# Trunk of two hybrid decoder layers: rows of `ar` copied on chip, loads kept back by a second planning run, another matmul order in the outer quarters

## The chip, the core and the metric

The kernel runs on one NeuronCore of a Trainium2 chip, as a single launch. The metric is the time of one execution on the device in microseconds. The core's engines are TensorE (PE; its weight loads are PEld), VectorE (DVE), ScalarE (ACT), GpSimd (POOL) and SyncE (SP). SyncE computes nothing here: it issues most of the DMAs, GpSimd issues the others.

## What is computed

One inference step of a trunk of two layers, for a prompt of 256 tokens and 8 sampled tokens (264 columns), model width 2048:

```python
h = rms_norm(x, norm_w)
z = jnp.einsum('btd,dc->btc', h, w_in)          # 2048 -> 7296 columns, all branches
y_a, ... = rwkv_time_mix(z_a, ...)              # A: 12 heads x 64, delta-rule state
y_b, ... = attention_branch(z_b, ...)           # B: dilated sliding windows, 12 heads x 64
y_c, ... = pool_branch(z_c, ...)                # C: causal mean pooling, 4 x 128 channels
y = x + jnp.einsum('btc,cd->btd', concat(y_a, y_b, y_c), w_out)
```

Branch A is a recurrence over tokens, `S = S * w + sa (kk * a)^T + v k^T`, read by `r`. The kernel computes it for the prompt in four chunks of 64 tokens. Outputs are the two activations, the recurrent states and the new key and value rows.

## The kernel before

**The stream.** All weights pass once through the core in float32. `stream` (L301) computes two output tiles of 128 columns at a time, a *pair*, for all 264 tokens. A pair has four *quarters* of the depth; for each quarter `load` (L294) brings 512 KB into `raw` (three buffers), ScalarE casts it to `hi` (two buffers, float32r) and VectorE forms the remainder `lo` (three buffers). A tile is then the sum of hi x xh, hi x xl (8 matmuls a quarter) and lo x xh (4 matmuls a quarter) in one PSUM bank `acc`. There are three such banks, so the second tile of a pair reuses the bank of the first tile of the pair before. In each quarter the order is: hi of tile 0, hi of tile 1, lo of tile 0, lo of tile 1. `scaled` (L327) evicts a finished bank on VectorE by a product with `rstd` into `z` (and `compb`), which releases it. There are 29 pairs or single tiles a layer for w_in, then 8 pairs for w_out in quarter order (2, 1, 3, 0).

**Branch A beside the stream.** `a_kdone` and `a_r` build the operands `bk` and `ar`: `ar` holds for each pair of heads, chunk and token 64 columns of r and 64 of minus kk, scaled by the decays. `a_solve` (L469) multiplies them into the masked blocks `gs`, stores these to the DRAM tensor `g_dram`, gathers the diagonal blocks (`xm`), and inverts 16x16 triangles on VectorE in 15 steps (`tm`, `rm`), with many small stores in between (`x_dram`, `ra_dram`, `rat_dram`, `rb_dram`, `rbt_dram`). L500 to L504 also store the second half of `ar` over those rows of `g_dram` where a head's block has no use for its own masked values. `invert` (L523) loads the pieces again and completes the inverse. `a_chain` then runs over the four chunks: `fetch` (L636) loads one chunk's `gs` (768 KB, two buffers) from `g_dram`, and `chunk` (L680) uses it as the weights of a product with `uv`; since the `ar` rows stand in `gs`, the state's part and the chunk's part are one matmul. Chunk 0 has no state and reads only the other rows of `gs`. Meanwhile the sampled tokens (`a_sample`) store and load rows through `sk_dram` and `sv_dram` (loads `svec`, `sval`).

**The order.** All instructions are first written down in program order; `Plan` then sets the order of each engine's queue. `Plan.run` (L1532) simulates a list schedule: for each engine the ready instruction with the longest remaining tail goes next, with estimated durations (`cost`), crossing times, buffers (`rings`: the tiles of one tag take their buffers in order) and a model of the DMA engines (`bus`, L1501). Each engine then executes its list in that order, and waits only for what it depends on. All SyncE DMAs, the weights of the stream among them, form one such list.

Of the kernel before, what the change touches and what calls it, by code (L numbers as in the profile page):

```python
# [19 lines left out]
P = 128  # L20
# [3 lines left out]
T = NP + NB  # L24
# [18 lines left out]
UROWS = (slice(0, 64), slice(64, 128))  # L43
# [60 lines left out]
class Trunk:  # L104
# [196 lines left out]
    def stream(self, w, c0, nt, xh, xl, order=(0, 1, 2, 3), begin=False):  # L301
        n = nt * P
        accs = [self.ps("acc") for _ in range(nt)]
        for q in order:
            if begin:
                self.first_x(q)
                xh, xl = self.xh, self.xl
            raw = self.early.pop(0) if self.early else self.load(w, c0, n, q)
            hi = self.wpool.tile([P, 4, 256], F32R, tag="hi", name=self.nm("hi"), bufs=2)
            lo = self.wpool.tile([P, 4, 256], F32R, tag="lo", name=self.nm("lo"), bufs=3)  # L310
            self.act(hi[:, :, :n], raw[:, :, :n])
            self.tt(lo[:, :, :n], raw[:, :, :n], hi[:, :, :n].bitcast(F32), ALU.subtract)
            parts = ((hi, xh), (hi, xl)), ((lo, xh),)
            for late, products in zip((False, True), parts):
                for t in range(nt):
                    cs = slice(t * P, (t + 1) * P)
                    for k4 in range(4):
                        k = 4 * q + k4
                        for i, (a, b) in enumerate(products):
                            first = q == order[0] and k4 == 0 and not late and i == 0  # L320
                            self.nc.tensor.matmul(accs[t][:, :T], a[:, k4, cs], b[k], start=first, stop=q == order[3] and k4 == 3 and late)  # L321
        return accs

    def project(self, tiles):
# [144 lines left out]
    def a_solve(self):  # L469
# [7 lines left out]
        for t0 in (0, 3):  # L477
            gs = [ap.tile([P, NH, P], F32, tag="gs", name=self.nm("gs"), bufs=2) for _ in UROWS]
# [8 lines left out]
            for par, g in enumerate(gs):  # L487
                g0 = par * 6 + t0
# [3 lines left out]
        n = 96  # L492
# [4 lines left out]
                         self.g_dram[r0:r0 + 32, 6 * par:6 * par + 6, :, c0:c0 + 32].rearrange("s t c x -> (t c) s x"))  # L497
        self.dma(self.x_dram, xm[:n, :1024])
        self.load_x()
        for par, hr in enumerate(UROWS):  # L500
            for t0 in (0, 3):
                g0 = par * 6 + t0
                self.dma(self.g_dram[hr, g0:g0 + 3].rearrange("p t c n -> p (t c) n")[:, :, 64:128],
                         self.ar[hr, t0:t0 + 3].rearrange("p t c n -> p (t c) n")[:, :, 64:128])  # L504
        view = lambda a: a[:n].rearrange("p (u x) -> p u x", u=2)[:, :, :512].rearrange("p u (s t) -> p u s t", t=32)[:, :, :, :16]
        X, R = view(xm), view(rm)
        self.nc.vector.memset(rm, 0.0)
# [128 lines left out]
    def fetch(self, cidx):  # L636

        gs = self.apool.tile([P, NH, P], F32, tag="gs", name=self.nm("gs"), bufs=2)
        self.dma(gs, self.g_dram[:, :, cidx, :])
        return gs  # L640

    def inverses(self):
# [684 lines left out]
def width(a, first=1):  # L1327
    n = 1
    for _, c in list(a.ap)[first:]:
        n *= c  # L1330
    return n


class Plan:


    def __init__(self, tc, bundles):
        self.tc = tc
        self.tiles = {t.name: t for t in tc.tiles}
        self.block = tc.nc.cur_bb.bb  # L1340
        self.masks = {}
        engine = lambda i: ENGINES.get(str(i.engine).split(".")[-1])
        self.ins = [i for i in self.block.instructions if engine(i) and not type(i).__name__.startswith("BassTilePool")]
        self.eng = [engine(i) for i in self.ins]
        self.n = len(self.ins)
        self.dma = [type(i).__name__ == "InstDMACopy" for i in self.ins]
        self.stream = [type(i).__name__ == "InstMatmult" and self.tiles[list(i.outs)[0].bass_ap.tensor.name].tag.startswith("acc") for i in self.ins]
        self.first = self.stream.index(True)
        self.dur = [self.cost(i, e) for i, e in zip(self.ins, self.eng)]
        self.port = [self.shares(i, e) for i, e in zip(self.ins, self.eng)]  # L1350
        self.dependences()
        self.bundle(bundles)
        self.rings()
        gone, self.phases = [], []
        for i in self.block.instructions:
            if type(i).__name__.startswith("BassTilePool"):
                op, pool = self.boundary(i)
                if op == "alloc":
                    self.phases += [(pool, g) for g in gone]
                else:  # L1360
                    gone.append(pool)
# [139 lines left out]
    def bus(self, i):  # L1501
        o = list(i.outs)[0]
        run = min(a.ap[-1][1] * 4 if a.ap[-1][0] == 1 else 4 for a in list(i.ins) + list(i.outs))
        return width(o, 0) * 4 * (1.0 if run >= 512 else 2.0 if run >= 128 else 2.46 if run >= 64 else 8) / 360.0


    def tails(self, factor, hop, loose=()):
# [21 lines left out]
                tail[q] = max(tail[q], t)  # L1529
        return tail  # L1530

    def run(self, factor=1, hop=300, margin=200, batch=0, wait=0, switch=0, quiet=0, lead=1, dyn=()):  # L1532
        n, eng, preds, dma, dur, stream = self.n, self.eng, self.preds, self.dma, self.dur, self.stream
        spare = {t: d for t, r in self.ring.items() for m, d in dyn if t.split("_" + self.pool[r[0]])[0] == m}
        tail = self.tails(factor, hop, spare)
# [2 lines left out]
        feeds = {q for k in range(n) if stream[k] for q in preds[k]}  # L1538
# [3 lines left out]
        count = [0] * n  # L1542
# [19 lines left out]
        open_tiles = Counter(self.pool[t] for t in left)  # L1562
        live = set()
        parked = defaultdict(list)
        est = [0.0] * n
        names = ("PE", "SIDE", "DVE", "ACT", "POOL", "SP")
        ready = {e: [] for e in names}
        queue = lambda k: "SIDE" if eng[k] == "PE" and not stream[k] else eng[k]
        pending = [(0.0, k) for k in range(n) if count[k] == 0]
        heapq.heapify(pending)  # L1570
        free = {e: 0.0 for e in names if e != "SIDE"}
        hw = bus_free = now = 0.0
        start, fin, order = [0.0] * n, [0.0] * n, {e: [] for e in free}
# [33 lines left out]
        while done < n:  # L1607
            while pending and pending[0][0] <= now + 1e-9:
                _, k = heapq.heappop(pending)
                heapq.heappush(ready[queue(k)], (prio[k], k))  # L1610
            while release and release[0][0] <= now + 1e-9:
                _, t = heapq.heappop(release)
# [5 lines left out]
            for e in free:  # L1618
                if free[e] > now + 1e-9 or (e == "SP" and hw > now + 700):
                    continue  # L1620
                if e == "PE" and forced is not None:
                    k = forced
                elif e == "PE":
# [3 lines left out]
                    k = None  # L1627
                    if h:
                        go = side_on or h[0][0] < -2e9 or now - since >= wait or sum(dur[x[1]] for x in h) >= batch
                        if go:  # L1630
                            k = take(h)
# [3 lines left out]
                    if k is None:  # L1635
                        k = take(ready["PE"])
                        if k is None and h:
                            k = take(h)
# [3 lines left out]
                else:  # L1642
                    k = take(ready[e])
# [55 lines left out]
            c = [x for x in free.values() if x > now + 1e-9]  # L1699
# [6 lines left out]
            c = [x for x in c if x > now + 1e-9]  # L1706
# [71 lines left out]
def build(nc, shapes, depth=DEPTH):  # L1778
    ins = {n: nc.dram_tensor(f"in_{n}", s, F32, kind="ExternalInput").ap() for n, s in shapes.items()}
    outs = {n: nc.dram_tensor(f"out_{n}", s, F32, kind="ExternalOutput").ap() for n, s in _OUTS}  # L1780
    with tile.TileContext(nc, schedule_with_timeline_sim=True) as tc, ExitStack() as ctx:
        trunk = Trunk(ctx, tc, ins, outs, depth)
        trunk.run()
        plan = Plan(tc, trunk.bundles)
        plan.run(switch=105, margin=350, hop=180, factor=0.9, lead=25, quiet=60, dyn=[("a", 2)])
        plan.apply()


# [10 lines left out]
```

## Time and profile before

| | us |
|---|---|
| median of 3 runs | 1103.1 (1100.97 to 1105.57) |
| the profiled execution | 1103.96 |
| its span, first to last instruction | 1102.2 |
| TensorE busy | 1052.2 (95%) |
| VectorE busy | 854.1 (77%) |
| ScalarE busy | 545.0 (49%) |
| mean granted TensorE clock | 0.986 of full |
| moved by DMA | 223.64 MB, 203 GB/s over the span |

Matmuls are pipelined, so a busy time close to the span says that TensorE is seldom without work, not that each matmul is at its shortest. "L137 ACT hi<-raw" is an instruction of ScalarE from line 137 (a helper that many steps share) that writes tile `hi` and reads tile `raw`. A gap on an engine is shown as the idle time before an instruction with the instruction that ended it. A DMA on SyncE's queue has the time that its issue held the queue, not that of its transfer.

### The profile page before, as it was taken

How to read it: one execution, taken by the hardware profiler on the slowest of the kernel's cores; microseconds unless marked ns; L12 is line 12 of the kernel's file. 1: busy time of each engine (PE TensorE's matmuls, PEld its weight loads, DVE VectorE, ACT ScalarE, POOL GpSimd, SP SyncE). 2: the span in 40 equal slices, each digit the busy share in tenths (PEclk: the TensorE clock that was granted, in tenths of full speed). 3: DMA queues.
4: the chain of work that ended last, by engine and by line, in shares of the span. 5: the costliest groups of instructions: out<-in, count | busy, mean ns of one | idle time of the engine just before them, and what ended most of it. 6: DMA issues, size and time to landing. Idle time of an engine off the chain costs nothing. (4 is left out here: it accounts for less than half of the span.)

```text
span 1102.2 us, 24582 instructions
## 1 busy us (share of the span) xinstructions
PE 1052.2 (95%) x9802; PEld 1001.2 (91%) x9802; DVE 854.1 (77%) x1684; ACT 545.0 (49%) x934; POOL 128.3 (12%) x262
## 2 busy tenths in 40 slices
PE   9999998889999999999999999979999989999998
PEld 8899898789998888999999998978899988799998
DVE  7769977689997987765665799668999889776443
ACT  7646533354745563444455464324565555544332
POOL 0002300101122100000100032001021211100000
PEclk9999999899999999999999999998999999999999
DMA  8654478977568845677765545898865687456774
GB/s 278 201 170 149 135 248 224 240 191 226 149 204 243 278 127 192 190 221 219 236 215 182 169 144 171 229 240 238 225 202 166 194 266 230 160 169 190 232 225 146
DMA packets 154683, 223.64 MB, mean 203 GB/s; under 512 B 75984, under 2 KB 109152, under 8 KB 154552
## 3 DMA queue, kind: packets, MB, share of 16 engines
q1 hardware_dynamic: 146456, 195.94, 59.2%
q0 software_dynamic: 8112, 26.12, 7.2%
q8 instruction: 77, 1.26, 0.5%
q14 instruction: 38, 0.31, 0.1%
HBM read 198.55 MB, written 24.03 MB: 202 GB/s over the span
## 5 line engine op out<-in xcount | busy, mean ns | idle before, releaser
L137 ACT ACTIVATE hi<-raw 128x1024 fp32r<-128x1024 f32 (+1 forms) x296 | 309.8, 1047 | 400.9 <-PE acc L321 259.2
L321 PE MATMUL acc<-xh,hi 128*128 128x264 f32 x1824 | 473.3, 291 | 27.3 <-ACT hi L137 12.6
L140 DVE TENSOR_TENSOR lo<-raw,hi 128x1024 fp32r<-128x1024 f32 (+1 forms) x296 | 357.4, 1208 | 158.9 <-ACT hi L137 156.9
L321 PE MATMUL acc<-xl,hi 128*128 128x264 f32 x1824 | 472.0, 291 | 0.0
L321 PEld LDWEIGHTS acc<-xh,hi 128*128 128x128 f32 x1824 | 347.7, 191 | 36.6 <-ACT hi L137 14.3
L321 PEld LDWEIGHTS acc<-xl,hi 128*128 128x128 f32 x1824 | 348.4, 191 | 6.3 <-issue 4.2
L321 PE MATMUL acc<-xh,lo 128*128 128x264 f32 x1824 | 278.8, 290 | 0.4 <-DVE lo L140 0.4
L321 PEld LDWEIGHTS acc<-xh,lo 128*128 128x128 f32 x1824 | 243.8, 191 | 4.4 <-issue 1.2
L140 DVE TENSOR_TENSOR z<-acc,rstd 128x264 f32<-128x264 f32 (+1 forms) x112 | 50.8, 463 | 17.2 <-PE acc L321 15.3
L321 PE MATMUL acc<-mb,hi 128*128 128x264 f32 x384 | 54.4, 284 | 0.0
L321 PEld LDWEIGHTS acc<-mb,hi 128*128 128x128 f32 x384 | 49.9, 188 | 0.0
L321 PE MATMUL acc<-ml,hi 128*128 128x264 f32 x192 | 48.5, 284 | 0.0
L321 PE MATMUL acc<-mh,hi 128*128 128x264 f32 x192 | 48.4, 283 | 0.0
L351 POOL COPY zcol<-z 128x9 f32<-128x9 f32 x50 | 17.9, 360 | 189.1 <-DVE z L140 187.4
L321 PEld LDWEIGHTS acc<-mh,hi 128*128 128x128 f32 x192 | 36.1, 188 | 0.0
L321 PEld LDWEIGHTS acc<-ml,hi 128*128 128x128 f32 x192 | 36.1, 188 | 0.0
L321 PE MATMUL acc<-mc,hi 128*128 128x264 f32 x256 | 34.4, 285 | 0.1
L321 PEld LDWEIGHTS acc<-mc,hi 128*128 128x128 f32 x256 | 32.3, 188 | 0.6 <-DVE mc L140 0.5
L321 PE MATMUL acc<-mb,lo 128*128 128x264 f32 x192 | 31.1, 284 | 0.0
L321 PE MATMUL acc<-mh,lo 128*128 128x264 f32 x192 | 31.1, 284 | 0.0
L140 DVE TENSOR_TENSOR xs<-acc,res 128x264 f32<-128x264 f32 x32 | 13.7, 429 | 20.2 <-PE acc L321 20.1
L321 PEld LDWEIGHTS acc<-mh,lo 128*128 128x128 f32 x192 | 26.5, 188 | 0.0
(357 smaller groups left out, 1302.7 us busy)
## 6 DMA issues: line engine op xcount, KB each, us to landing
raw<-in_w_in SPq DMA_DIRECT2D x224, 512.0 KB
raw<-in_w_out SPq DMA_DIRECT2D x64, 512.0 KB
g_dram<-gs SPq DMA_DIRECT2D x8, 768.0 KB
gs<-g_dram SPq DMA_DIRECT2D x8, 768.0 KB
kc<-in_cache_k_w POOLq DMA_DIRECT2D x12, 512.0 KB, 7.3
qb<-q_dram SPq DMA_DIRECT2D x12, 512.0 KB
vc<-in_cache_v_w POOLq DMA_DIRECT2D x12, 512.0 KB, 4.6
s<-in_state_wkv POOLq DMA_DIRECT2D x12, 256.0 KB, 4.4
```

Of the source, the lines that this page charges most:

```text
L137: self.nc.scalar.activation(out, in_, func, **kw)
L140: self.nc.vector.tensor_tensor(out, a, b, op=op)
L321: self.nc.tensor.matmul(accs[t][:, :T], a[:, k4, cs], b[k], start=first, stop=q == order[3] and k4 == 3 and late)
L351: self.nc.gpsimd.tensor_copy(self.zcol[:, :, a], z[:, NP - 1:T])
```

## The change

There are three edits.

1. The four DMAs a layer that store `ar` into `g_dram` are gone. Instead, `fetch` copies the 64 columns from `ar` into the loaded `gs` on ScalarE, two copies a chunk, for chunks 1 to 3.
2. `Plan.run` can plan twice. With `ahead` the first run gives, for each DMA into SBUF that isn't a `raw` load, the earliest start among the instructions that read it; in the second run the DMA isn't ready until 12,000 ns before that. The estimate for transfers in runs of 512 to 1023 bytes rises from 1.0 to 1.25.
3. In `stream`, in the first and the last quarter of a pair, the matmuls are sorted by tile: hi and lo of tile 0, then hi and lo of tile 1. The two middle quarters stay as they were.

```diff
             parts = ((hi, xh), (hi, xl)), ((lo, xh),)
-            for late, products in zip((False, True), parts):
-                for t in range(nt):
-                    cs = slice(t * P, (t + 1) * P)
...
+            turns = [(late, t) for late in (0, 1) for t in range(nt)]
+            if q in (order[0], order[3]):
+                turns.sort(key=lambda x: x[1])
+            for late, t in turns:
+                cs = slice(t * P, (t + 1) * P)
...
         self.dma(self.x_dram, xm[:n, :1024])
         self.load_x()
-        for par, hr in enumerate(UROWS):
-            for t0 in (0, 3):
-                g0 = par * 6 + t0
-                self.dma(self.g_dram[hr, g0:g0 + 3].rearrange("p t c n -> p (t c) n")[:, :, 64:128],
-                         self.ar[hr, t0:t0 + 3].rearrange("p t c n -> p (t c) n")[:, :, 64:128])
...
         self.dma(gs, self.g_dram[:, :, cidx, :])
+        for par, hr in enumerate(UROWS):
+            if cidx:
+                self.act(gs[hr, 6 * par:6 * par + 6, 64:128], self.ar[hr, :, cidx, 64:128])
         return gs
...
+        self.first_out = [list(i.outs)[0].bass_ap.tensor.name if d else None for i, d in zip(self.ins, self.dma)]
+        self.after_load = defaultdict(list)
+        for k in range(self.n):
+            for q in self.preds[k]:
+                if self.dma[q] and self.first_out[q] in self.tag and not self.dma[k]:
+                    self.after_load[q].append(k)
...
-        return width(o, 0) * 4 * (1.0 if run >= 512 else 2.0 if run >= 128 else 2.46 if run >= 64 else 8) / 360.0
+        return width(o, 0) * 4 * (1.0 if run >= 1024 else 1.25 if run >= 512 else 2.0 if run >= 128 else 2.46 if run >= 64 else 8) / 360.0
...
+        self.hold = [0.0] * self.n
+        args = factor, hop, margin, batch, wait, switch, quiet, lead, dyn
+        if ahead:
+            self.once(*args)
+            for k, i in enumerate(self.ins):
+                if self.dma[k] and not self.feeds(k):
+                    self.hold[k] = max(0.0, min([self.start[q] for q in self.after_load[k]], default=0.0) - ahead)
+        return self.once(*args)
+
+    def feeds(self, k):
+        return self.tag[self.first_out[k]].startswith("raw") if self.first_out[k] in self.tag else False
...
-        est = [0.0] * n
+        est = list(self.hold)
...
-        pending = [(0.0, k) for k in range(n) if count[k] == 0]
+        pending = [(est[k], k) for k in range(n) if count[k] == 0]
...
-        plan.run(switch=105, margin=350, hop=180, factor=0.9, lead=25, quiet=60, dyn=[("a", 2)])
+        plan.run(ahead=12000, switch=105, margin=350, hop=180, factor=0.9, lead=25, quiet=60, dyn=[("a", 2)])
```

`once` is the former `run`. The transfers that part 1 removes have runs of 64 elements (256 bytes).

## Rows read from the trace of the kernel before

**Rows 1.** The page, busy time, share of the span and instructions of each engine
```profile
PE 1052.2 (95%) x9802; PEld 1001.2 (91%) x9802; DVE 854.1 (77%) x1684; ACT 545.0 (49%) x934; POOL 128.3 (12%) x262
```

**Rows 2.** Waits of TensorE: for whom, us in total, times, longest
```profile
PE acc L321 <- ACT hi L137: 12.6, 8, 4.3
PE acc L321 <- DVE z L140: 8.8, 13, 2.1
PE acc L321 <- DVE compb L140: 6.0, 5, 2.5
...
PE acc L321 <- DVE lo L140: 0.4, 1, 0.4
```

**Rows 3.** Windows: length, busy us of PE, PEld, DVE, ACT, POOL (x), clock, DMA share, GB/s
```profile
184.00:187.00 3.00, 2.98 (x14) 3.00 (x15) 2.93 (x6) 1.69 (x3) 0.00 (x0) 0.50 0.69 194
...
194.00:204.00 10.00, 5.35 (x34) 4.66 (x34) 2.43 (x6) 2.75 (x4) 0.86 (x2) 0.83 1.00 239
...
500.00:525.00 25.00, 25.00 (x209) 25.00 (x208) 15.91 (x23) 12.26 (x19) 2.70 (x5) 1.00 0.76 233
...
740.00:752.00 12.00, 7.96 (x43) 7.43 (x43) 6.89 (x11) 5.09 (x6) 1.08 (x2) 0.72 1.07 250
...
744.00:750.00 6.00, 5.03 (x23) 5.03 (x24) 4.12 (x4) 4.95 (x6) 0.54 (x1) 0.50 1.13 296
```

**Rows 4.** Timeline of TensorE: start, us, instruction, [idle before, who ended it]
```profile
180.34 0.39 PE L321 MATMUL acc<-xh,hi 128*128 128x264 f32 x1 [1.46 <-ACT hi L137]
...
184.03 0.56 PE L321 MATMUL acc<-xh,hi 128*128 128x264 f32 x1 [2.45 <-DVE compb L140]
...
202.33 0.59 PE L321 MATMUL acc<-xh,hi 128*128 128x264 f32 x1 [4.32 <-ACT hi L137]
...
727.17 0.36 PE L321 MATMUL acc<-xh,hi 128*128 128x264 f32 x1 [2.45 <-DVE compb L140]
...
744.97 0.59 PE L321 MATMUL acc<-xh,hi 128*128 128x264 f32 x1 [3.72 <-ACT hi L137]
```

**Rows 5.** Timeline of SyncE's queue, 174 to 198 us
```profile
174.40 1.46 SPq L155 DMA_DIRECT2D raw<-in_w_in  x1
...
176.38 3.50 SPq L155 DMA_DIRECT2D g_dram<-ar  x4
179.97 0.63 SPq L155 DMA_DIRECT2D raw<-in_w_in  x1
...
187.18 0.38 SPq L155 DMA_DIRECT2D raw<-in_w_in  x1
187.65 1.51 SPq L155 DMA_DIRECT2D gs<-g_dram  x2
189.25 5.42 SPq L155 DMA_DIRECT2D ra_dram<-rm  x2
...
196.13 1.50 SPq L155 DMA_DIRECT2D raw<-in_w_in  x1
```

**Rows 6.** Timeline of ScalarE in the same stretch, casts that waited for weights
```profile
179.23 1.06 ACT L137 ACTIVATE hi<-raw 128x1024 fp32r<-128x1024 f32 x1 [4.45 <-DMA raw<-in_w_in]
...
201.22 1.06 ACT L137 ACTIVATE hi<-raw 128x1024 fp32r<-128x1024 f32 x1 [8.38 <-DMA raw<-in_w_in]
```

**Rows 7.** Groups by line: shapes, count, busy us, mean ns, idle before
```profile
L137 ACT ACTIVATE uv<-st 64x384 f32<-64x384 f32 x12 | 6.3, 521 | 2.3 <-DVE st L140 2.0
...
L140 DVE TENSOR_TENSOR lo<-raw,hi 128x1024 fp32r<-128x1024 f32 (+1 forms) x296 | 357.4, 1208 | 158.9 <-ACT hi L137 156.9
```

**Rows 8.** Timeline of TensorE, first matmuls that read a fetched gs
```profile
238.19 0.92 PE L115 MATMUL a<-uv,gs 64*64 64x64 f32 x24
```

**Rows 9.** Waits of ScalarE's casts for TensorE
```profile
ACT hi L137 <- PE acc L321: 259.2, 153, 4.8
```

**Rows 10.** Timeline of TensorE, 908 to 920 us
```profile
912.77 0.39 PE L321 MATMUL acc<-xh,hi 128*128 128x264 f32 x1 [2.06 <-DVE z L140]
```

More of the change, by code (lines that the diff above doesn't have):

```diff
@@ L313, in stream @@
             parts = ((hi, xh), (hi, xl)), ((lo, xh),)
-            for late, products in zip((False, True), parts):
-                for t in range(nt):
-                    cs = slice(t * P, (t + 1) * P)
[L317 to L321, printed above, removed]
+            turns = [(late, t) for late in (0, 1) for t in range(nt)]
[3 more added lines that the diff above has]
+                cs = slice(t * P, (t + 1) * P)
+                for k4 in range(4):
+                    k = 4 * q + k4
+                    for i, (a, b) in enumerate(parts[late]):
+                        first = q == order[0] and k4 == 0 and not late and i == 0
+                        self.nc.tensor.matmul(accs[t][:, :T], a[:, k4, cs], b[k], start=first, stop=q == order[3] and k4 == 3 and late == 1)
         return accs
@@ L1530, in tails, with run, once @@
         return tail
-    def run(self, factor=1, hop=300, margin=200, batch=0, wait=0, switch=0, quiet=0, lead=1, dyn=()):
+    def run(self, factor=1, hop=300, margin=200, batch=0, wait=0, switch=0, quiet=0, lead=1, dyn=(), ahead=0):
+        self.hold = [0.0] * self.n
[8 more added lines that the diff above has]
+        return self.tag[self.first_out[k]].startswith("raw") if self.first_out[k] in self.tag else False
+    def once(self, factor, hop, margin, batch, wait, switch, quiet, lead, dyn):
         n, eng, preds, dma, dur, stream = self.n, self.eng, self.preds, self.dma, self.dur, self.stream
```

## Prediction

> **What bounds the kernel now.** I read the busy times first: TensorE is busy for 1052.2 of 1102.2 us, VectorE for 854.1, ScalarE for 545.0 [rows 1]. The kernel is therefore a TensorE kernel, and a change can only win time in the 50 us in which TensorE stands still and in stretches where its clock is low. Next I read TensorE's own waits [rows 2]: 12.6 us for the ScalarE cast `hi`, 8.8 and 6.0 us for the VectorE evictions `z` and `compb` that free an accumulator, and next to nothing (0.4 us) for `lo`. Third come the windows [rows 3], which tell where. In an undisturbed stretch TensorE runs 209 matmuls in 25 us, so one every 0.120 us, with the 16 DMA engines 0.76 busy. From 194 to 204 us it runs 34 in 10 us with the DMA share at 1.00, and from 740 to 752 us 43 in 12 us at 1.07: this is the same place in both layers, the triangular solve of branch A (pairs 29-30 and 31-32). I call it the crunch. Fourth, TensorE's timeline there [rows 4]: stalls of 1.46, 2.45 and 4.32 us in layer 0, of 2.45 and 3.72 us in layer 1, 14.4 us in all, mostly for `hi`.
>
> Why `hi` is late is read from ScalarE's timeline [rows 6]: it waited 4.45 and 8.38 us for weights (`raw`). Why the weights are late is read from SyncE's queue [rows 5], which issues every `raw` load in one line with all else. Its slices stand back to back: four `ar` stores take 3.50 us just ahead of the `raw` at 179.97; two `gs` loads (1.51 us) are followed by two small `ra` stores that hold the queue for 5.42 us, and the next `raw` goes out only at 196.13. The cast that needs it starts at 201.22 and TensorE at 202.33. The `gs` loads that stand in the way at 187.65 are first read by a matmul at 238.19 [rows 8], 50 us later.
>
> After the stalls the granted clock is 0.50, the 1.2 GHz level [rows 3]: 14 matmuls from 184 to 187 us, where 25 fit at the full rate (1.3 us lost), and 23 from 744.97 to 750, 5.03 us for what takes 2.75 (2.3 us lost). Layer 0 has a second dip like the latter behind the 4.32 us stall; I put it at 2.3 too. The crunch thus costs 14.4 + 5.9 = 20.3 us.
>
> **Part 1, `ar` by a copy.** Removed: eight stores of 192 KB, four a layer, 3.50 us of SyncE's queue each time [rows 5], and their DMA time. Added: for chunks 1 to 3, two ScalarE copies of 64x384 each, 12 in all. The same form exists (`uv<-st`, 521 ns [rows 7]): 12 x 0.521 = 6.3 us of an engine that is idle half the time. Bounds 0 (beside idle time) and 6.3 (all in front of a needed cast); nearer to 0, since ScalarE waited 259.2 us in 153 waits for TensorE to release a `hi` buffer [rows 9], 1.7 us each, so a copy of half a microsecond usually stands in such a wait. I take **+1**. It adds a wait: the copy waits for the landing of `gs`, and behind it on ScalarE stand the casts, for which TensorE waits. That is the slower rival below.
>
> **Part 2, loads kept back.** The planner runs once, and then no SBUF load but `raw` may go earlier than 12 us before its first reader started in that run. Stores have no hold. In the crunch this moves the eight `x` loads, `svec`, `sval` and the `gs` loads behind several `raw` loads. For `gs` one step more is needed: the first reader of chunk 0's is the matmul at 238, so it is held to about 226. Those of chunks 1 to 3 are first read by the new copy, which follows the landing at once, so their own hold is idle; but the two `gs` buffers are taken in order, so chunk 1's can't pass chunk 0's. Loads issued by GpSimd are held as well; its queue was no bottleneck at 128.3 us busy [rows 1]. The changed bus price (1.25 for runs of 512 to 1023 bytes) only shifts the order.
>
> What goes: with `ar`, `gs` and the small loads out of the way, the `raw` of 179.97 can go some 3.5 us and that of 196.13 some 10 us sooner, more than the stalls of 4.32 and 3.72 us. I count both and their two dips: 8.0 + 4.6 = **-12.6**. What stays: the stall of 1.46 us, whose `raw` was issued at 174.40, ahead of all that is removed, and the dip of 1.3 us. What is late next are the small stores, which keep their place.
>
> What comes: two `gs` loads of 768 KB near 226 us. At the 239 GB/s of the crowded window [rows 3] they are 6.4 us of all DMA engines a layer. The bounds are 0 (three `raw` buffers hide it) and 12.8 for both layers; SyncE's queue is emptier there, so I stay near the lower end: **+3**.
>
> The Trainium skill speaks against this part: "DMA: Bandwidth & Descriptors", Rules for kernel authors, says to issue a DMA early and wait for its semaphore late, so that its fixed cost overlaps with work. By that rule the two `gs` loads at 187.65 were placed well and part 2 would win nothing. The trace differs so far: the 5.42 us of queue behind them is the price of the early issue.
>
> **Part 3, tiles completed early.** In the first and last quarter of a pair the order hi t0, hi t1, lo t0, lo t1 becomes hi t0, lo t0, hi t1, lo t1. Tile 0's sum ends 8 matmuls sooner (12 before the end, not 4), and the next pair's second tile, which needs that buffer of three, starts after 12 matmuls and not 8. The eviction gets 12 x 0.120 = 1.44 us more. Behind one `lo` (1.21 us on VectorE [rows 7]) it now just gets through. The waits for `z` and `compb` are 14.8 us in 18 [rows 2]. Two of them are the 2.45 us in the crunch: 1.44 off each, **-2.9**. The other 16 sum to 9.9, 0.6 each, less than the slack but for the one of 2.06 us [rows 10], where 0.6 is left. At most 9.3 are to be had, at least 0, if the planner spends the slack on other work; I take **-5**, the middle, as some stand at a pair's start, where the order gives nothing.
>
> Its price: `lo` is wanted 0.96 us sooner in outer quarters. The cast runs ahead [rows 9], and TensorE waited for `lo` once, 0.4 us, in the crunch [rows 2]. Bounds 0 and 3.8 (two quarters in each crunch); **+0.4**. A `hi` buffer is released 4 matmuls (0.5 us) later in those quarters, inside the 1.7 us wait: 0.
>
> **Sum.** -12.6 - 2.9 - 5 + 1 + 3 + 0.4 = -16.1 us. The profiled execution took 1104.0 us (span 1102.2 and 1.8 around it), so 1087.9; from the median, 1103.1, it is **1087**. The profiled execution lies within the runs shown, 0.9 above their median.
>
> **Rivals.** (a) *The crunch stays.* Small stores (`sk`, `x_dram`, `ra`, `rb`, `rat`) keep SyncE's queue as full, and the weights are late as before. For it: the `raw` of 174.40 itself took 1.46 us to issue before any `ar` or `gs`. Against: the 5.42 us come right behind `gs`. This is also where the rule of the Trainium skill above would lead. Then only part 3 pays: 1103.1 - 7.9 + 4.4 = 1100.
> (b) *ScalarE is held by a late `gs`.* Six copies wait for a load that the planner believes landed; in order behind them stand the casts. Cover 1.7 us [rows 9]. If the loads come late as `raw` did in the crunch, by 8.38 us [rows 6], each costs 6.7, six 40, and against the gain 1127; at 6.6 us late it is 4.9 each, 29 in all: 1116. It decides from 2.7 us beyond cover (16 / 6), where the gain is gone. For it: the new place of `gs` is crowded too. Against: 12 us ahead is more than 1.5 MB need (6.4 us).
> (c) *More goes than counted.* With the queue free, the stall of 1.46 us, the last dip and all evictions go, and nothing comes: 20.3 + 9.3 = 29.6, less 1 for the copies: 1074.
>
> **Chances.** Forecast (1080 to 1095) 0.55; (a) 0.22; (c) and better 0.13; (b) 0.10. The range reaches from 1070, a little below (c), to 1104, which takes in (a) and the costs of `gs` at their bound (1087 + 9.8 = 1097); it leaves out (b) and the far end of (c). A measurement of this kernel tells about 0.5% (5.5 us) from no change, so faster means below 1097.6: forecast, (c) and a fourth of (a), 0.74; within 0.5% the rest of (a), 0.16; slower 0.10.
>
> **What the changed profile would show.** Right: no `g_dram<-ar`; `gs` loads issued within some 15 us of their chunk; no wait of ScalarE over 3 us for `raw` between 185 and 205 us; TensorE's waits for `z` and `compb` together under 8 us; clock 1.00 where it was 0.50 at 744. Wrong: ScalarE waits named `gs<-g_dram`, TensorE waiting for `lo`, or `raw` late at 220 to 240 us. The forecast falls if the new order, which the planner draws up afresh for the whole kernel, opens stalls elsewhere.

## The result, and the profile after

The change makes the kernel a little slower. Six runs of the changed kernel have a median of 1110.9 us (1102.8 to 1111.5), six of the kernel before beside them 1102.9 us; the ratio, of the means 1108.9 and 1103.1, is 1.0053, 95% interval 1.0029 to 1.0078. The forecast was 1087. The six runs of the changed kernel lie in two groups, two at 1103 to 1106, the profiled one among them, and four near 1111; why isn't known.

The profiled execution of the changed kernel took 1105.99 us, its span is 1104.2 us. The page's line of busy times, to be held against [rows 1]:

```profile
PE 1054.3 (95%) x9802; PEld 1003.3 (91%) x9802; DVE 857.1 (78%) x1684; ACT 551.7 (50%) x946; POOL 131.2 (12%) x262
```

TensorE does the same 9802 matmuls; ScalarE has its 12 copies more. What changed shows in the waits of TensorE (for whom, us in total, times, longest), to be held against [rows 2]:

```profile
PE a L115 <- DMA vc<-in_cache_v_w: 8.4, 4, 3.6
PE a L115 <- issue: 6.9, 5, 4.2
PE a L118 <- DVE compb L140: 6.7, 3, 3.6
PE a L118 <- DVE z L140: 5.8, 5, 4.5
PE a L115 <- POOL comp L465: 2.5, 2, 1.2
PE acc L323 <- ACT hi L137: 2.2, 4, 1.0
PE acc L323 <- DVE lo L140: 1.1, 2, 0.7
```

The stream's waits ahead of its own matmuls (`acc`) for `hi` (12.6), `z` (8.8) and `compb` (6.0) are all but gone: 2.2 for `hi`, none listed for the other two. In their place TensorE stands ahead of matmuls of the branches (`a`): 12.5 us ahead of the transposes that read `z` and `compb`, 8.4 us for `vc`, the cached values of branch B, and 6.9 us for which the profile names nothing ("issue"). I added up all gaps of TensorE over 0.15 us by the instruction that follows: before 27.7 us ahead of stream matmuls and 17.9 ahead of the others, after 3.3 and 42.6. The sums are 45.6 and 46.0 us. **The stalls were not removed but moved**, all 24 us of them. Within the span the granted clock stood at 0.50 for 37.5 us, before for 31.1.

**The crunch after the change.** The windows of [rows 3] (columns as there: length, busy us of PE, PEld, DVE, ACT, POOL, clock, DMA share, GB/s):

```profile
184.00:187.00 3.00, 3.00 (x27) 3.00 (x26) 0.93 (x2) 2.02 (x3) 0.00 (x0) 1.00 0.65 177
194.00:204.00 10.00, 5.47 (x35) 5.26 (x34) 6.05 (x10) 4.26 (x5) 0.00 (x0) 0.80 0.53 187
500.00:525.00 25.00, 25.00 (x208) 25.00 (x207) 16.25 (x23) 12.88 (x20) 2.70 (x5) 1.00 0.77 232
740.00:752.00 12.00, 8.36 (x49) 8.14 (x48) 8.15 (x14) 4.96 (x6) 0.00 (x0) 0.72 0.46 145
```

From 194 to 204 and from 740 to 752 us the DMA engines are relieved (0.53 and 0.46, before 1.00 and 1.07), yet TensorE runs 35 and 49 matmuls where it ran 34 and 43. The reason is one engine further on. Timeline of VectorE in layer 0 (start, us, instruction, [idle before, who ended it]):

```profile
192.80 0.17 DVE L140 TENSOR_TENSOR compb<-acc,rstd 128x8 f32<-128x8 f32 x1
197.91 0.69 DVE L140 TENSOR_TENSOR s<-s,svec 128x512 f32<-128x512 f32 x1 [4.94 <-issue]
198.64 0.69 DVE L152 TENSOR_REDUCE asa<-s 128x8 f32<-128x512 f32 x1
199.24 1.22 DVE L140 TENSOR_TENSOR lo<-raw,hi 128x1024 fp32r<-128x1024 f32 x1
200.37 0.58 DVE L140 TENSOR_TENSOR z<-acc,rstd 128x256 f32<-128x256 f32 x1
```

GpSimd's, which issues the state that VectorE reads at 197.91:

```profile
190.63 0.57 POOL L158 DMA_DIRECT2D s<-in_state_wkv  x1 [20.91 <-DMA rb_dram<-rm]
```

And TensorE's:

```profile
196.20 0.28 PE L323 MATMUL acc<-xh,lo 128*128 128x264 f32 x1
201.01 0.69 PE L118 MATMUL a<-cbase,z 128*128 128x128 f32 x2 [4.53 <-DVE z L140]
```

VectorE's list puts the first product of the sampled tokens (`s<-s,svec`) ahead of a `lo` and a `z` of the stream. It reads a recurrent state that GpSimd issued at 190.63, as soon as the store of `rm` had freed its buffer; by the trace's record of that DMA it landed 7.20 us later, at 197.83. (The profile itself names "issue" as what ended the wait; that it was the state is read from this landing, 0.08 us before the product.) VectorE stands for 4.94 us, the `z` behind it comes at 200.37, and TensorE, whose next instruction is the transpose of that `z`, stands for 4.53 us. Layer 1 does the same (state issued at 737.02, with the profile naming a `raw` load as what ended the wait; it landed after 5.64 us, VectorE idle 4.55 until 742.73, TensorE 3.65 until 743.98). The 4.32 and 3.72 us of [rows 4] have come back as 4.53 and 3.65, and the clock falls behind them as before.

The state had company. SyncE's queue issued three `raw` loads in a row around it, the first 0.6 us ahead:

```profile
190.03 2.49 SPq L155 DMA_DIRECT2D raw<-in_w_in  x3
```

From 190.63 to 197.83 the 16 DMA engines were 0.87 busy and moved 297 GB/s, which is 2.1 MB, as much as the three `raw` loads and the two states that GpSimd issued then. In layer 1 three `raw` loads went out from 735.86 on, and from 737.02 to 742.65 the share was 0.98. So the crowd at the DMA engines was not gone; it stood a few us earlier, around the state.

**Why the planner did that.** It takes a load that GpSimd issues as begun 1.69 us after the issue, or later where its model of the bus is taken, then its time on the bus (0.73 us for 256 KB, 1.46 for 512 KB, by the code's 360 bytes a ns), then 0.91: 3.3 us for a state, 4.1 for `vc`. The DMA issues of the changed kernel (KB each, median us from issue to landing) say otherwise:

```profile
vc<-in_cache_v_w POOLq DMA_DIRECT2D x12, 512.0 KB, 5.2
s<-in_state_wkv POOLq DMA_DIRECT2D x12, 256.0 KB, 5.5
```

And those of the kernel before:

```profile
vc<-in_cache_v_w POOLq DMA_DIRECT2D x12, 512.0 KB, 4.6
s<-in_state_wkv POOLq DMA_DIRECT2D x12, 256.0 KB, 4.4
```

On a free bus the plan believes the state 2.2 us sooner than the median lands, and the queues, which run in order, wait for it. It was too early in the kernel before as well, by 1.1 us for a state and 0.5 for `vc`, but there the first product ran at 208.95, 11 us later. The two stalls behind the states (8.2 us) and the waits for `vc` (8.4, before 2.1) make up 14.5 of the 24.7 us that came ahead of the other matmuls. The Trainium skill, "DMA: Bandwidth & Descriptors", Anatomy of one DMA — SWDGE (gpsimd) path, has a fit of some 2 us plus the bytes at 436 GB/s; for 256 KB that would be 2.6 us, an estimate from that page. The trace differs, 5.5 us under this kernel's load, and the measurement decides.

### The profile page after: what moved, and what is told of

It is laid out like the page before. It is cut to its first block, busy times and chain, and to the rows that moved or that the text cites. A ratio compares the mean times of both kernels' runs of the same rounds, so it can differ in the third digit from the quotient of the medians.

```text
span 1104.2 us, 24588 instructions
## 1 busy us (share of the span) xinstructions
PE 1054.3 (95%) x9802; PEld 1003.3 (91%) x9802; DVE 857.1 (78%) x1684; ACT 551.7 (50%) x946; POOL 131.2 (12%) x262
## 4 chain that ended last, share of the span: by engine, by line
PE 42%; DVE 11%; DMA 6%; issue 2%; ACT 1%; POOL 0%; SPq 0%; DVEq 0%; ACTq 0%; POOLq 0%
PE acc L323 37%; DVE lo L140 3%; PE a L115 3%; DMA raw<-in_w_in 2%; DMA vc<-in_cache_v_w 2%; PE a L118 1%; DVE s L140 1%; DMA svec<-sk_dram 1%; ACT hi L137 1%; DVE z L140 1%; DMA i_dram<-iv 1%; DMA rwkv_a_up<-in_rwkv_a_up 1%; DVE bk L149 0%; DVE kc L140 0%; DVE bk L140 0%
## 5 line engine op out<-in xcount | busy, mean ns | idle before, releaser
L323 PE MATMUL acc<-xh,lo 128*128 128x264 f32 x1824 | 300.4, 291 | 1.2 <-DVE lo L140 1.1
L323 PEld LDWEIGHTS acc<-xh,lo 128*128 128x128 f32 x1824 | 252.5, 191 | 8.9 <-issue 4.2
L323 PE MATMUL acc<-mb,hi 128*128 128x264 f32 x384 | 57.0, 284 | 0.0
L353 POOL COPY zcol<-z 128x9 f32<-128x9 f32 x50 | 20.9, 418 | 210.4 <-DVE z L140 209.4
L140 DVE TENSOR_TENSOR s<-s,svec 128x512 f32<-128x512 f32 x36 | 24.7, 686 | 13.7 <-issue 4.9
L323 PE MATMUL acc<-mb,lo 128*128 128x264 f32 x192 | 33.8, 285 | 0.0
L323 PE MATMUL acc<-mh,lo 128*128 128x264 f32 x192 | 33.6, 283 | 0.0
```

What stands on the lines that cost most here:

```text
L140: self.nc.vector.tensor_tensor(out, a, b, op=op)
L353: self.nc.gpsimd.tensor_copy(self.zcol[:, :, a], z[:, NP - 1:T])
```

## Experiments

**Theories.** A: the plan believes loads of GpSimd landed too early, and the in-order queues then stand for them; with a truer landing the change pays. B: what was gained in the stream is lost because the plan packs TensorE's evictions more tightly (part 3's slack is spent). C, formed later: a fresh plan of the whole kernel differs from the last by chance, by more than the change is worth.

### One part at a time

> Part 1 alone (no ar stores, two ScalarE copies a chunk), one planning run, old matmul order. Theory A (what is taken out of the crunch is given back where an in-order engine reaches an instruction whose load the planner believes landed): the gs loads still go out some 50 us early, so the raw load behind them stays late and TensorE still stands 2 to 4 us for hi near 200 us; 1098 to 1105, TensorE idle in all 40 to 48 us. Theory B (the holds are what costs, the other two parts win what I forecast): part 1 wins its share of the queue, 1097 to 1101. Theory C (any new plan scatters by some us): anything within 6 us of before, with no pattern in where it stands.

The edit, on the kernel before (the four stores are taken out as well):

```diff
+        for par, hr in enumerate(UROWS):
+            if cidx:
+                self.act(gs[hr, 6 * par:6 * par + 6, 64:128], self.ar[hr, :, cidx, 64:128])
```

Measured 0.9996 (0.9966 to 1.0027), no change. The stores are gone, TensorE's gaps sum to 45.8 us as before. The `gs` loads did not go out 50 us early, as expected, but 70 us: they no longer have the stores to wait for, and stand at 164.41 and 166.76. The two `ra` stores take 0.89 us, and the stalls for `hi` near 202 and 745 us are gone by this part alone. In their place TensorE stands 4.33 and 3.43 us for `compb`, behind a VectorE that already waits 3.05 and 2.11 us for states:

```profile
201.77 0.56 PE L321 MATMUL acc<-xh,hi 128*128 128x264 f32 x1 [4.33 <-DVE compb L140]
...
745.25 0.56 PE L321 MATMUL acc<-xh,hi 128*128 128x264 f32 x1 [3.43 <-DVE compb L140]
```

> Part 2 alone (second planning run with 12 us of hold, new bus price), ar stores kept, old matmul order. Theory A: the wait for hi near 200 us is gone, because gs goes out near 225 us; in its place VectorE waits 3 to 5 us for the state load s, or TensorE for a side operand; 1098 to 1108. Theory B: slower than before by 5 to 10 us (1108 to 1113), with waits for x and vc that before hasn't got. Theory C: within 6 us of before.

On the kernel before, the second planning run and the new bus price:

```diff
+        return width(o, 0) * 4 * (1.0 if run >= 1024 else 1.25 if run >= 512 else ...
+        plan.run(ahead=12000, switch=105, ...
```

0.9991 (0.9963 to 1.0019). The 12.6 us of the stream's waits for `hi` are all gone. Gaps ahead of the stream fall from 27.7 to 15.8 us, those ahead of other matmuls rise from 17.9 to 31.0: the move of the changed kernel, half of it, from this part alone.

> Part 3 alone (tile order in the outer quarters), one planning run, ar stores kept. Theory A and theory B both: the waits for z and compb before stream matmuls fall from 14.8 us to under 5; theory B lets the time fall with them, 1093 to 1098; theory A moves them to side matmuls, with TensorE's idle time still 42 to 48 us and 1099 to 1106. Theory C: within 6 us of before.

```diff
+            if q in (order[0], order[3]):
+                turns.sort(key=lambda x: x[1])
```

1.0047 (1.0019 to 1.0075). TensorE's waits in it:

```profile
PE acc L323 <- ACT hi L137: 14.5, 5, 7.0
PE a L115 <- DMA vc<-in_cache_v_w: 5.8, 3, 3.9
PE a L115 <- DMA rt<-i_dram: 4.3, 4, 1.4
PE a L118 <- DVE compb L140: 4.0, 2, 2.0
```

One wait of the stream for `z` is left, 1.2 us, where [rows 2] have 14.8 us for `z` and `compb`: the slack of part 3 was real and larger than counted. But 5.4 us came back ahead of the transposes of the two (4.0 for `compb`, 1.4 for `z`), and the crunch got worse, two stalls in its timeline of TensorE where [rows 4] have 4.32 and 3.72:

```profile
199.86 0.59 PE L323 MATMUL acc<-xh,hi 128*128 128x264 f32 x1 [6.01 <-ACT hi L137]
...
744.78 0.59 PE L323 MATMUL acc<-xh,hi 128*128 128x264 f32 x1 [6.99 <-ACT hi L137]
```

> The changed kernel with one planning run only (parts 1 and 3 and the new bus price, no hold). Theory B: the waits for x (1.6 us) and vc (8.4 us) fall back to before's 2 us, and it is faster than before, 1092 to 1098. Theory A: gs goes out early again, the wait for hi near 200 us comes back in part, the other waits stay; 1099 to 1108. Theory C: within 6 us of the changed kernel, either way.

```diff
-        plan.run(ahead=12000, switch=105, ...
+        plan.run(switch=105, ...
```

Parts 1 and 3, with the new bus price: 1.0005 (0.9975 to 1.0035); 14.0 us of waits for `hi` are back. They are not those of before. The `gs` loads are out of the way (164.66 and 170.50), the `ra` stores take 0.95 us, and the longest single wait is 3.0 us. SyncE's queue still has the eight `x` loads (5.04 us from 183.26) and four loads of `invert` (194.93 to 202.30) between the `raw` loads, which stand from 204 to 218 us in the changed kernel; that they cause these waits is likely and not shown.

> Parts 1 and 2 without part 3. Since part 3 alone cost 0.47% and parts 1 and 2 alone nothing that can be told from zero, theory A' (part 3 is what costs; it adds no slack because the planner puts the transposes that read z forward by the same 8 matmuls): 1102 to 1106, so about as before, with waits for z and compb back before stream matmuls. Rival (the hold costs when it meets the copy): as slow as the changed kernel, ratio 1.004 to 1.007 to before.

The changed kernel with the old loop of `stream` put back, so parts 1 and 2: 0.9969 (0.9933 to 1.0005). The waits of the stream for `z` (10.8) and `compb` (6.3) are back, as theory B has it, but the time is no worse than with part 3; its expectation of 1102 to 1106 us was met (1102.7).

Taken by themselves these five say that no part gains, and that part 3 costs half a per cent. The runs further down show that this reading is not to be trusted: each is one plan.

### The landing of GpSimd's loads

> The changed kernel, and the planner believes that a GpSimd-issued load begins 5.0 us after its issue and not 1.69 (so a state load s lands after 6.6 us in the plan; 7.2 was measured near 190 us). Nothing else differs. Theory A (in-order engines stand before loads that the plan believes landed): VectorE's waits of 4.9 and 4.6 us before the first s product at 198 and 743 us fall under 1 us, TensorE's waits there (4.5 and 3.6) and for vc (8.4 in all) fall below 2 each, and the time falls by 8 to 14 us against the changed kernel, to 1095 to 1102. Rival (the DMA engines are full there, where TensorE stands is only bookkeeping): the waits move to other names, the time stays within 3 us of the changed kernel.

```diff
-                        begin = max(now + 1690, bus_free)
+                        begin = max(now + 5000, bus_free)
```

Only the planner's belief changes, and with it the order. 1086.7 us, **0.9809 (0.9764 to 0.9854)**, a larger gain than the 8 to 14 us expected. VectorE around the place at which it stood:

```profile
198.26 0.17 DVE L140 TENSOR_TENSOR compb<-acc,rstd 128x8 f32<-128x8 f32 x1
198.34 0.68 DVE L140 TENSOR_TENSOR s<-s,svec 128x512 f32<-128x512 f32 x1
```

The product follows the eviction without a gap, since the plan now lets `z`, `lo` and `compb` go first. The waits for `vc` are gone from TensorE's list, and its gaps sum to 36.7 us, 9.3 less than in the changed kernel. Theory A holds for what stood there. That the time meets the forecast of 1087 is chance, as the next run shows.

> The kernel before, with the same longer GpSimd landing in the plan and nothing else. It has no wait of VectorE for s in the crunch, only 2.1 us for vc. Theory A: 0 to 3 us faster than before. Rival (a new plan scatters by several us whatever is altered): anything within 6 us of before.

The same line in the kernel before: 0.9867 (0.9822 to 0.9913). Both expectations, 0 to 3 us faster and within 6 us, are missed. The landing also pays without the change, so most of the 1.9% is not the change's. It removes nothing that [rows 2] show for the stream (`hi` 13.4, `z` 6.0, `compb` 6.7); the gaps ahead of other matmuls fall from 17.9 to 12.7, those for `vc` from 2.1 to 0.8.

> The changed kernel, and the planner takes 1.4 us more from a stream matmul to whatever on another engine reads its sum, the time that part 3 was to win. Theory A': the plan no longer spends the slack, TensorE's waits named z and compb before its transposes fall from 12.5 us to under 4 and the time by 4 to 9 us against the changed kernel. Rival (VectorE is late by more than that, behind a late load): the waits before the transposes at 201 and 744 us stay at 3 us or more, the time within 3 us of the changed kernel.

```diff
-                        r += slack[q]
+                        r += slack[q] + (1400 if stream[k] else 0)
```

0.9926 (0.9895 to 0.9956) with the short landing. A margin of 1.4 us between a stream matmul and what other engines read of it. TensorE's waits for `z` and `compb` ahead of transposes went from 12.5 us to none, as theory A' of the expectation has it, and the time fell by 1.3% (0.9926 / 1.0053), more than its 4 to 9 us. But the waits went back ahead of the stream (`compb` 9.7, `z` 6.7), and VectorE still stands 2.42 and 5.18 us for states. Theory A alone doesn't give that: a plan with the late states left in it ran faster. How much of it is the margin's and how much the new plan's, one plan can't tell.

> Parts 1 and 2 with the longer landing (5000 ns for loads that GpSimd issues) in the planner, without part 3. With all three parts and the longer landing it was 0.981 of the kernel before, with none of the three 0.987. If part 3 pays once the plan knows when state loads land, this kernel stands with the latter, 0.986 to 0.990, and TensorE waits some 10 us before stream matmuls for z and compb, as without part 3 before. If part 3 is worth nothing or costs (it cost 0.5% alone), this one stands at 0.976 to 0.981.

The changed kernel with the longer landing and the old loop of `stream`: 1082.3 us, 0.9782 (0.9746 to 0.9818), in the range of a part 3 that is worth nothing or costs.

> Parts 1 and 3 with the longer landing in the planner, without the second planning run. If part 2 carries the gain of the three parts under the longer landing, this kernel is at 0.986 to 0.990 of the kernel before and TensorE waits over 10 us for hi, most of it in the crunch (near 200 and 745 us). If part 2 is worth nothing, it is at 0.979 to 0.983.

The changed kernel with the longer landing and `ahead` left out: 1083.5 us, 0.9807 (0.9758 to 0.9856). Waits for `hi` are 12.3 us again, which part 2 had removed, and it costs nothing that can be measured: the range of a part 2 that is worth nothing. With the longer landing all three parts, the first two, and the first and third stand at 0.981, 0.978 and 0.981: no part can be told to carry the gain.

### The same kernels, planned afresh

One weight of the planner (`switch`, the cost in ns of a change of accumulator) is moved from 105 to 108 or 102. It is a small move, but the greedy planner then draws up a different order for every engine.

> The changed kernel with one weight of the planner moved a little (the cost of a change of accumulator 108 in place of 105), so that the order of every engine is drawn up afresh with the same three parts. If the 0.5% that the change lost belongs to its parts, this kernel is at 1.001 to 1.009 of the kernel before, VectorE again stands over 3 us ahead of the product that reads the late state load, and stalls before the transposes remain. If it is only the luck of one plan, it can be anywhere between 0.99 and 1.01, and differences of half a per cent between plans say nothing of the parts.

```diff
-        plan.run(ahead=12000, switch=105, ...
+        plan.run(ahead=12000, switch=108, ...
```

The changed kernel, planned again: 1092.5 us, **0.9879 (0.9838 to 0.9920)**, 1.7% faster than the changed kernel. The expectation from the parts (1.001 to 1.009) is wrong; that from the plan's luck is the nearer one, though its range ended at 0.99. The windows of its crunch:

```profile
194.00:204.00 10.00, 9.30 (x75) 9.09 (x76) 10.00 (x18) 4.99 (x6) 0.00 (x0) 1.00 0.50 116
740.00:752.00 12.00, 9.37 (x156) 9.13 (x155) 10.04 (x20) 4.31 (x8) 2.65 (x5) 0.91 0.98 224
```

75 matmuls in the first window, where both kernels have 34 or 35, at clock 1.00. VectorE also waits for a state here, 3.17 us at 191.68, but with less of the stream behind it: TensorE's only stall over 0.3 us between 190 and 205 is 1.53 us. In layer 0 this is what part 2 was forecast to do. In layer 1 the second window has other work in it, as this plan has the `ra` stores at 714.20 and not at 732.63; there VectorE waits 4.12 us, until 725.35, and TensorE behind it 2.51 us, until 728.32. A late state costs TensorE as much as the plan happens to have put behind it.

> The same small move of the planner's weight (108 for 105) with the longer landing of 5000 ns. If the 1.9% that the longer landing gave belongs to the landing and not to the luck of one plan, this kernel is at 0.976 to 0.987 of the kernel before, at least 1% ahead of the replanned kernel without it, and VectorE does not wait over 1 us for a state load. If it was luck, it stands within 0.5% of the replanned kernel without it.

The same with the longer landing: 1071.9 us, **0.9695 (0.9660 to 0.9731)**, the fastest kernel of this study and below the expected range (0.976 to 0.987). The same two windows:

```profile
194.00:204.00 10.00, 10.00 (x84) 10.00 (x84) 10.00 (x17) 5.46 (x7) 0.21 (x1) 1.00 0.61 185
740.00:752.00 12.00, 12.00 (x274) 11.65 (x273) 11.69 (x26) 5.24 (x9) 1.61 (x3) 1.00 1.15 240
```

TensorE does not stand at all in these windows; in this plan's solve, which in layer 1 again comes earlier (`ra` stores at 711.24), its stalls are one of 1.45 us, until 183.61, and one of 0.44. Its gaps over the whole kernel sum to 24.7 us.

The remaining six fill a table of three weights, with and without the change, with both landings. Their edits are the two lines already shown, `switch` at 102 or 108 and, where the label has "late", 5000 for 1690, in the kernel that the label names:

> The kernel before with the planner's weight moved from 105 to 108, nothing of the change. If the 1.7% by which the replanned changed kernel beat the changed one is the luck of a plan, the kernel before moves as freely, anywhere from 0.985 to 1.015 of itself, and the gain or loss of the change can only be read as a mean over several plans. If 108 is simply the better weight, this one is at 0.982 to 0.990 like the changed kernel at 108. If the change itself is what 108 brought out, this one stays within 0.997 to 1.003.

> The kernel before with 102 in place of 105. Luck of a plan: 0.985 to 1.015. A weight that is better the higher it is: 1.005 to 1.015. A plan that hardly cares: 0.997 to 1.003.

> The changed kernel with 102 in place of 105. With the three plans of each kernel the change is judged by the mean of its three ratios (so far 1.005 and 0.988) against the mean of the three of before. If the forecast's mechanism was right and only this one plan spoiled it, this one is below 0.995. If the changed kernel is worth nothing on average and 108 was luck, it is at 0.998 to 1.012.

> The kernel before with 108 and the longer landing of 5000 ns. If the landing gives what it gave at 105 (1.3%) whatever the plan, it is 0.010 to 0.016 below the kernel before at 108. If that gain was the luck of a plan, the difference is within 0.005 of nothing or of the other sign.

> The kernel before with 102 and the longer landing of 5000 ns. A gain of the landing: 0.010 to 0.016 below the kernel before at 102. Luck of a plan: within 0.005 of it, or above.

> The changed kernel with 102 and the longer landing of 5000 ns. A gain of the landing: 0.015 to 0.025 below the changed kernel at 102, and 0.003 to 0.015 below the kernel before with the landing at 102, as at 105 and, so far, at 108. Luck of a plan: within 0.005 of the changed kernel at 102, or above.

Ratios to the kernel before on the same chip, with their intervals:

| weight | before | changed | before, longer landing | changed, longer landing |
|---|---|---|---|---|
| 102 | 1.0062 (1.0032 to 1.0092) | 0.9913 (0.9876 to 0.9951) | 0.9917 (0.9890 to 0.9943) | 0.9764 (0.9723 to 0.9805) |
| 105 | 1 | 1.0053 (1.0029 to 1.0078) | 0.9867 (0.9822 to 0.9913) | 0.9809 (0.9764 to 0.9854) |
| 108 | 1.0000 (0.9966 to 1.0033) | 0.9879 (0.9838 to 0.9920) | 0.9966 (0.9937 to 0.9995) | 0.9695 (0.9660 to 0.9731) |
| mean | 1.0021 | 0.9948 | 0.9917 | 0.9756 |

Against the expectations: the kernel before at 108 did not move (1.0000), and at 102 by 0.6%, so it scatters less than the changed kernel; the changed kernel at 102 is below 0.995, where "only this one plan spoiled it" puts it. The longer landing gains 0.3% at 108 in the kernel before, which is the range of luck, and 1.5% at 102 in both kernels, which is that of a gain.

What the table says, in differences of its cells:

- **The change.** Six pairs: -1.5, +0.5, -1.2, -1.5, -0.6 and -2.7 points, mean -1.2, with an interval from their scatter of -2.3 to 0.0. Five of six point to a gain, so on the mean there probably is one, but the interval of six pairs ends at none; the plan that was measured as the result is the one with a loss.
- **The landing.** Six pairs: -1.5, -1.3, -0.3, -1.5, -2.4, -1.8, mean -1.5, interval -2.2 to -0.8. It gains in every one, in the kernel before too, where no VectorE wait for a state is over 2.3 us; TensorE's waits for `vc` go there (3.1, 2.1 and 2.7 us to 0, 0.8 and 0).
- **The weight.** The means of the three rows (with 1 for the kernel before) are 0.991, 0.993 and 0.989. No weight is the better one; 108 is no improvement found by chance.
- **The plan.** Cells of one column differ by 0.6 to 1.7 points without a change in the work.

The same twelve by TensorE's gaps over 0.15 us in each profile, ahead of stream matmuls + ahead of others, and in brackets VectorE's longest idle time ahead of a product with a state:

| weight | before | changed | before, longer landing | changed, longer landing |
|---|---|---|---|---|
| 102 | 24.2 + 23.5 (1.20) | 3.2 + 37.1 (3.52) | 25.2 + 13.5 (under 1) | 4.0 + 26.2 (under 1) |
| 105 | 27.7 + 17.9 (under 1) | 3.3 + 42.6 (4.94) | 26.6 + 12.7 (under 1) | 4.8 + 31.9 (under 1) |
| 108 | 27.0 + 22.0 (2.29) | 3.5 + 32.4 (4.12) | 25.9 + 12.0 (under 1) | 3.7 + 21.0 (under 1) |

This separates what the change does from what the plan does. In all six pairs the change takes 21 to 24 us of stalls away from the stream, whatever the plan. In all six it puts 9 to 25 us ahead of other matmuls; how many, and so the sign of the result, is the plan's doing, and the plan that was measured has the most. With the short landing VectorE stands over 3 us for state products in each changed plan and in none of before (in the plan of 108 the 4.12 us are put down to `sval`, another load of the sampled tokens, the 3.17 us to a state); with the longer landing none of the six has such a wait over 1 us, and 5 to 11 us of the gaps ahead of other matmuls go.

Over all 20 kernels of this study, each part does to the stream what it was meant to do. With the second planning run the stream's waits for `hi` are 0 to 2.2 us, without it 7.5 to 14.8; with the new matmul order its waits for `z` and `compb` are 0 to 1.6 us (except with the margin of 1.4 us, 16.4), without it 10.7 to 17.1. Where the time goes instead is what the plans differ in. The gaps are also not all of it: the granted clock was 0.50 for 31.1 us in the kernel before, for 37.5 in the changed one and for 14.7 to 27.3 in the other five changed plans of the table.

## Why the prediction was wrong

**What bounds the kernel** was read rightly in the main: TensorE with 45 us of gaps, the crunch in both layers, and the SyncE queue as the cause of the longest waits for weights. In the changed kernel the two `ra` stores that held the queue for 5.42 us [rows 5] take 1.09 us, as its timeline of SyncE's queue has it:

```profile
184.36 0.38 SPq L155 DMA_DIRECT2D svec<-sk_dram  x1
184.79 1.09 SPq L155 DMA_DIRECT2D ra_dram<-rm  x2
185.92 1.84 SPq L155 DMA_DIRECT2D rb_dram<-rm  x1
```

But part 1 by itself does this too, and the `gs` loads were not all of the cause: with parts 1 and 3 they are out of the way, and 14.0 us of waits for `hi` remain.

**Part 1, +1.** Nothing speaks against the size, and no run measures it alone. The copies take 0.51 to 0.53 us each, and the longest wait of ScalarE for a `gs` is 0.78 us. Rival (b), ScalarE held by a late `gs`, didn't happen.

**Part 2, -12.6: the step that failed.** The weights came in time for TensorE and its stalls for `hi` in the crunch went, 8.0 us as counted. I asked what is late next, and answered: the small stores. It was a load on another engine's queue, the state, which GpSimd issues, in layer 0 once a small store, that of `rm`, had landed, and among three `raw` loads. I had looked at GpSimd's queue only for being busy (128.3 us, "no bottleneck"), not at how long its loads take to land against what the planner believes, though the trace of before shows 4.4 us for a state, 5.6 to 6.1 in the crunch, where the code has 3.3. The kernel stands at TensorE for what VectorE has in front of it, and the new plan put the late state there.

The sign I looked for, "no wait of ScalarE over 3 us for `raw` between 185 and 205 us", also failed: it waited 3.72 us, until 194.64. That is the seed of rival (a): small stores and `sval` hold the queue from 184.79 to 189.93, and the next `raw` goes out at 190.03. But TensorE did not wait for it; its stall came at 196.5, behind VectorE. Nor was the clock 1.00 where it had been 0.50 at 744: it was 0.54 from 744 to 750 us.

**The costs of `gs` at its new place, +3.** Bounds 0 to 12.8, or 13.2 with a KB of 1024 bytes. From 210 to 240 us the DMA share rose from 0.81 to 1.10 and the mean clock fell from 0.94 to 0.83, so the crowd did move there. With all else planned afresh I can't give it a price of its own.

**Part 3, -2.9 and -5: the mechanism right, the account incomplete.** All 14.8 us of the stream's waits for `z` and `compb` went, more than my bound of 2.9 + 9.3. What I named as the lower end, "at least 0, if the planner spends the slack on other work", is in part what the measured plan did: 12.5 us ahead of the transposes of `z` and `compb`, 0.5 before, of which 8.2 are the two stalls behind the late states. I took the middle between the ends without a reason to leave the lower one; in the other five changed plans of the table these waits are 4.6 to 9.0 us. **`lo`, +0.4**, measured 1.1.

**The missing term: the new plan.** I wrote that the forecast falls if the fresh order opens stalls elsewhere, and gave that neither a price nor a chance: a term put at nothing without a reason. It is as large as any other: 1.7 points are 19 us. The kernel before spans 0.6 points over three plans, the changed one 1.7. The range ended at 1104 because it summed the bounds of known costs; the scatter of a list that is drawn up afresh for 24,588 instructions belonged in it, and would have reached both sides of no change. With the short landing the changed kernel's plans of 102 and 108 stand at -0.9 and -1.2% where the forecast had -1.5%; in the third, the one measured, all that was won in the stream was given back. That the plan drawn was the worst of the three is bad luck; that a draw could do this is the term that was missing.

**What stays open.** Which of the three parts carries the mean gain in time: alone or in twos they were run on one plan each, and their differences (0.9969 to 1.0047 with the short landing, 0.978 to 0.981 with the longer one) are within the scatter of plans. The 5 to 11 us that TensorE waits in every changed plan for "issue", most of it at `a<-iv,y` products, have no cause that the profile shows. They come with part 2: the ten kernels with the second planning run have 5.1 to 10.8 us of it, the ten without 1.2 to 4.1.

## What to carry to other kernels

A change to a kernel whose order a greedy planner draws up is a change plus a new draw: measure it on several plans (move an unrelated weight a little) before a half per cent is put down to it, and put that scatter into the range. When stalls go in one place, sum TensorE's gaps over the whole kernel by what follows them, since in-order queues hand a stall on to whatever the next list puts behind the latest load. And hold the planner's landing times against the trace's: here one constant was worth 1.5% on average, no less than the three edits under study (1.2%).

## What the runs showed of the hardware that was not expected

A 256 KB load issued by GpSimd, which the code takes at 3.3 us, landed after 4.4 us (median, kernel before) to 5.5 us (changed kernel), and after 7.20 us in the crunch, with the DMA engines 0.87 busy while it ran. The two small `ra` stores hold SyncE's queue for 5.42 us behind two `gs` loads and 1.09 us without them. All runs agree: in the seven kernels that issue the `gs` loads just ahead, the two stores hold it for 5.0 to 6.3 us in either layer, in the other thirteen for 0.9 to 1.1.
